# First values' projection: low parts of the weights on VectorE, one-column operations on ScalarE, the norm's factor in SBUF, other row products moved into the attention

## The chip, the cores and the metric

The kernel runs on one core of a Trainium2 chip. The metric is the device time of one execution in microseconds (us). A core has five queues that matter here: TensorE (PE: matrix products, and PEld, the loading of their stationary operand), VectorE (DVE), ScalarE (ACT), GpSimd (POOL) and SyncE (SP), which issues the transfers from the chip's memory (HBM). SBUF is the working memory; PSUM holds the results of TensorE, in eight banks of 512 float32 columns on 128 partitions each.

## The reference

A trunk of four layers over 512 positions and 1024 features, in float32. Every sub-layer normalizes its input, scales and shifts it by factors from a conditioning vector `c`, and adds a gated, normalized result. The first sub-layer, where this change lies, is attention with 16 heads of 64:

```python
mod_all = jnp.einsum('bd,lde->lbe', jax.nn.silu(c), w_mod) + b_mod[:, None, :]
...
sh_m, sc_m, g_m, sh_f, sc_f, g_f = jnp.split(mod_all[layer], 6, axis=-1)
u = modulate(rms_norm(h, norm_g[layer, 0]), sh_m, sc_m)
...
q, k, v = jnp.split(u @ w_qkv, 3, axis=-1)
```

with `modulate(h, shift, scale) = h * (1 + scale) + shift`. Behind it come the 16 heads (scores, a cumulative product along the keys, weighted values), the output projection, and a channel mixer.

## The kernel before

**Number format.** Each float32 operand of a large product is split in two parts, `hi` (rounded by ScalarE) and `lo` (the rest, a subtraction, `split`, L235 to L238). A product is then three matmuls: hi with hi, hi with lo, lo with hi (`mm3`, L219 to L222). Weights arrive in a tile `raw` (four buffers, one 512 KB transfer each, issued by SP) and are split into `whi` and `wlo`, or, in the spare form, into two chunks each of tag `x`. ScalarE makes the high part; the low part is made by GpSimd where `far` (L172 to L174) says so, otherwise by VectorE. While `starting` is set, `far` says GpSimd, and the split is made in two halves.

**Row products.** A block of 128 elements of `mod_all` is a product of the 128 rows of a transferred 128x1024 block with `c`, summed along the row, by one VectorE operation (`mod_block`, L371 to L376). It uses the same four `raw` buffers.

**The start.** The kernel forms the norm's factor R of the input (`pre_r`, `rstd`): squares, two float32 products with `ones_d` into an `aux` bank of PSUM, and four short operations, the last of which (L429) writes R over that same bank. Then, for each of 8 blocks k of 128 features (`prenorm`, L453 to L473): `first(k)` makes the two row products of the block (shift and scale) and `mod_pre` their four one-column operations on VectorE (L384 twice, L385, L387); the weights of block k are fetched and split; VectorE scales `t` = h times `apre` times R (L466); ScalarE makes the high part of u (L467) and VectorE the low part (L469).

**The values' projection** (`attention`, `mid`, L670 to L682) accumulates V = u @ w_v over the 8 blocks in eight accumulators at once, four of tag `mm` and four of tag `aux`, which are all eight banks of PSUM: 24 matmuls per block, 192 in all. After each of the first six blocks one task is taken from a list (`self.some(V_SOME[k])`): a row product that is needed only later. Then follow projections of queries and keys for head pairs (`q_block`, `k_block`), 24 matmuls each, and the loop over the heads (`sticks`, `flip`, `gather`), in which one further task is taken per round (L726) and the rest at its end.

**Order.** Each engine works through its queue in order. The queues are filled at build time by a scheduler that follows the code's order and dependencies; inside the head loop TensorE's order is written out (`ordered`).

Of the kernel before, what the change touches and what calls it, by code (L numbers as in the profile page):

```python
# [11 lines left out]
AF = mybir.ActivationFunctionType  # L12
ALU = mybir.AluOpType
# [4 lines left out]
KC = D // P  # L18
S = 512
# [3 lines left out]
HEADS = 16  # L23
# [4 lines left out]
QT = 4  # L28
N_WARM = 60
H_TB, H_H = 1, 0  # L30
V_SOME = (1, 1, 1, 1, 1, 1, 0, 0)
NB = S // QT
NPAIR = 32
FULL = slice(0, S)
# [44 lines left out]
class Trunk:  # L79
    def __init__(self, ctx, tc, ins, out):  # L80
        self.tc, self.nc, self.ins, self.out = tc, tc.nc, ins, out
        nc = self.nc
        pool = lambda **k: ctx.enter_context(tc.tile_pool(**k))
        self.const = pool(name="const", bufs=1)
        self.act = pool(name="act", bufs=1)
        self.wp = pool(name="wp", bufs=3)
        self.tmp = pool(name="tmp", bufs=2)
        self.mx = pool(name="mx", bufs=1)
        self.ps = pool(name="ps", bufs=4, space=bass.MemoryType.PSUM)
        self.dram = pool(name="dram", bufs=1, space=bass.MemoryType.DRAM)  # L90
        self.n = 0
        self.todo = []
        self.halves = {}
        self.crossing = False
        self.ordered, self.last, self.mark = False, None, None
        self.hold = None
        self.joint, self.clock, self.starting, self.near = False, 0.0, True, False

        self.cb = self.const.tile([P, D], F32, name="cb")
        nc.sync.dma_start(self.cb, ins["c"].to_broadcast([P, D]))  # L100
        self.h = self.const.tile([P, KC, S], F32, name="h")
        for k in range(KC):
            nc.sync.dma_start(self.h[:, k, :], ins["xT"][:, k, :])
        self.vec = self.const.tile([P, VCOLS], F32, name="vec")
        nc.sync.dma_start(self.vec, ins["vec"])
        nc.vector.tensor_scalar(self.v("ln_g"), self.v("ln_g"), -0.5, None, ALU.mult)

        self.ident = self.const.tile([P, P], F32, name="ident")
        make_identity(nc, self.ident)
        self.ident_b = self.const.tile([P, P], BF16, name="ident_b")  # L110
        nc.vector.tensor_copy(self.ident_b, self.ident)
        self.ones_d = self.const.tile([P, P], F32, name="ones_d")
        nc.vector.memset(self.ones_d, 1.0 / D)
        mask = self.const.tile([P, P], F32, name="mask")
        nc.vector.memset(mask, -1e30)
        nc.gpsimd.affine_select(out=mask, in_=mask, pattern=[[1, P]], compare_op=ALU.is_ge,
                                fill=0.0, base=0, channel_multiplier=-1)
        self.mask_b = self.const.tile([P, P], BF16, name="mask_b")
        nc.vector.tensor_copy(self.mask_b, mask)
        self.zero = self.const.tile([P, 1], F32, name="zero")  # L120
        nc.vector.memset(self.zero, 0.0)
        self.epsb = self.const.tile([P, 1], F32, name="epsb")
        nc.vector.memset(self.epsb, EPS)

        warm = self.psum("aux")
        for _ in range(N_WARM):
            nc.tensor.matmul(warm[:, :P], self.ident_b, self.mask_b, start=True, stop=True)
        sig = self.wp.tile([P, D], F32, tag="raw", bufs=4, name="sig")
        nc.scalar.activation(sig, self.cb, AF.Sigmoid)
        nc.vector.tensor_tensor(self.cb, self.cb, sig, ALU.mult)  # L130
        self.mod = [self.const.tile([P, 48], F32, name=f"mod{l}") for l in range(DEPTH)]
        self.apre = [self.const.tile([P, 2, KC], F32, name=f"apre{l}") for l in range(DEPTH)]
        self.gpost = [self.const.tile([P, 2, KC], F32, name=f"gpost{l}") for l in range(DEPTH)]
# [37 lines left out]

    def far(self, i):  # L172

        return self.starting or self.ordered and not self.near and (i or not self.crossing)  # L174

    def fetch(self, src):
        raw = self.wp.tile([P, D], F32, tag="raw", name=self.nm("raw"), bufs=4)
# [3 lines left out]
    def weights(self, src, spare=None, raw=None):  # L181

        n = src.shape[-1]
        if raw is None:
            raw = self.fetch(src)
        if spare:
            t = [[self.chunk(spare) for _ in range((n + S - 1) // S)] for _ in range(2)]
            for i, (hi, lo) in enumerate(zip(*t)):
                w = min(S, n - i * S)
                self.split(raw[:, i * S : i * S + w], hi[:, :w], lo[:, :w], self.far(i))  # L190
            cut = lambda t: [t[k // 4][:, (k % 4) * P : (k % 4 + 1) * P] for k in range(n // P)]
            return cut(t[0]), cut(t[1]), t
        hi = self.wp.tile([P, D], F32R, tag="whi", name=self.nm("whi"))
        lo = self.wp.tile([P, D], F32R, tag="wlo", name=self.nm("wlo"))
        if self.ordered or self.starting:
            for i, c in enumerate((slice(0, n // 2), slice(n // 2, n))):
                self.split(raw[:, c], hi[:, c], lo[:, c], self.far(i))
        else:
            self.split(raw[:, :n], hi[:, :n], lo[:, :n])
        cut = lambda t: [t[:, k * P : (k + 1) * P] for k in range(n // P)]  # L200
        wide = lambda t: [t[:, i * S : (i + 1) * S] for i in range(2)]
        return cut(hi), cut(lo), (wide(hi), wide(lo))
# [176 lines left out]
    def mod_pre(self, l, s, k=0, n=KC):  # L379
# [6 lines left out]
                                       self.v("norm_g", (l * 4 + 2 * s) * KC + k, n), ALU.add, ALU.mult)  # L386
        nc.vector.tensor_scalar(self.apre[l][:, s, k : k + n], self.apre[l][:, s, k : k + n], -0.5, None, ALU.mult)  # L387

    def mod_gate(self, l, s):
        nc = self.nc  # L390
        e = 24 * s + 16
        o = VOFF["b_mod"][0] + 48 * l + e
        g = self.gpost[l][:, s, :]
        nc.vector.tensor_tensor(g, self.mod[l][:, e : e + 8], self.vec[:, o : o + 8], ALU.add)
        nc.vector.scalar_tensor_tensor(g, g, -0.5, self.v("norm_g", (l * 4 + 2 * s + 1) * KC, KC),
                                       ALU.mult, ALU.mult)
# [55 lines left out]

    def prenorm(self, l, s, u, sl=FULL, before=None):  # L453
        nc = self.nc
        R, _ = yield from self.pre_r(sl)
        n = sl.stop - sl.start
        room = self.psum("aux") if n < S else None
        for k in range(KC):
            if before is not None:
                before(k)  # L460
            if sl.start == 0:
                u.append((self.chunk("u"), self.chunk("u")))
            hi, lo = u[k][0][:, sl], u[k][1][:, sl]
            a, b = self.apre[l][:, s, k : k + 1], self.mod[l][:, 24 * s + k : 24 * s + k + 1]
            t = self.scratch("t", sl) if room is None else room[:, k % 2 * n : (k % 2 + 1) * n]
            scale = nc.vector.scalar_tensor_tensor(t, self.h[:, k, sl], a, R, ALU.mult, ALU.mult)  # L466
            self.step = nc.scalar.activation(hi, t, AF.Identity, bias=b), scale  # L467
            if k % 2 == 0 or not self.crossing:
                nc.vector.scalar_tensor_tensor(lo, t, b, hi.bitcast(F32), ALU.add, ALU.subtract)  # L469
            else:  # L470
                x = self.scratch("t", sl)
                nc.scalar.activation(x, t, AF.Identity, bias=b)
                nc.gpsimd.tensor_tensor(lo, x, hi.bitcast(F32), ALU.subtract)  # L473
# [152 lines left out]
    def attention(self, l, j, first=None, spare=(), n_p=4):  # L626
        nc, ins = self.nc, self.ins
# [42 lines left out]
        def mid():  # L670
            v = [self.pairs("hid", 3) + [(self.chunk("hid", F32),)] for _ in range(2)]
            pss = [self.psum("aux" if i % 2 else "mm") for i in range(8)]
            for k in range(KC):
                if n_s:
                    wv.append(self.weights(ins["sb_w_v"][j, k]))
                hi, lo = wv[k][2]
                for tb in range(4):
                    ts = slice(tb * P, (tb + 1) * P)
                    for half in range(2):
                        self.mm3(pss[2 * tb + half], u[k][0][:, ts], u[k][1][:, ts], hi[half], lo[half],  # L680
                                 k == 0, k == KC - 1)
                self.some(V_SOME[k])  # L682
            self.starting = False
            todo = [proj(i) for i in range(n_s, HEADS)]
            self.load(todo[0])
# [14 lines left out]
            it, n = iter(()), 0  # L700
            for i in range(HEADS + 2):
# [7 lines left out]
                if todo:  # L709
                    b = todo.pop(0)  # L710
                    it, n = self.steps(b), b["srcs"][0].shape[-1] // P
# [10 lines left out]
                if i >= HEADS - 2:  # L722
                    while 2 * len(os) + 1 <= i - 2:
                        os.append((self.chunk("x"), self.chunk("x")))
                        self.split(o[len(os) - 1], *os[-1])
                self.some(1)  # L726
            self.several(it, 1)
            self.ordered = False
            self.rest()
# [553 lines left out]
    def run(self, subs=8):  # L1283
        nc = self.nc

        def first(k):
            if k == 1:
                self.mark, self.hold = self.step[1], self.step
            self.mod_block(0, k)
            self.mod_block(0, 8 + k)  # L1290
            self.mod_pre(0, 0, k, 1)

        ph = []
        for l in range(DEPTH):
# [113 lines left out]
```

## Time and profile before

| | us |
|---|---|
| three timed executions | 2680.76, 2685.21, 2686.60 |
| their median | 2685.21 |
| the profiled execution | 2679.98 |
| its span in the profile | 2678.3 |

The profiled execution is one more execution, not one of the three. Its span runs from the first to the last instruction in the trace. All times of the rows below count from the start of that span. In a row, "busy" is the time in which an engine worked; the clause in brackets is the idle time of the engine just before the instruction, and what ended it. `L216` is line 216 of the kernel; names such as `aux`, `u`, `raw` are those of the tiles.

### The profile page before, as it was taken

To read this page: it belongs to the slowest core of one execution; us is meant where nothing else is said; L and a number is where in the kernel's file an instruction comes from. 1 tells how busy PE (TensorE), PEld (TensorE's weight loads), DVE (VectorE), ACT (ScalarE), POOL (GpSimd) and SP (SyncE) were. 2 spreads that over 40 slices of the span, in tenths; PEclk is the share of its full clock that TensorE was granted. 3 is DMA by queue.
4 is the path that set the end of the run, shared out by engine and by line. 5 is a ranking of instruction groups with operands and counts; after the bars stand their busy time and mean duration, and the time that the engine had idled before them with its cause. 6 is when DMAs were issued, how large, how long until landed. Compare 5 with 4: busy or idle time off the path is not lost. (4 is left out here: it accounts for less than half of the span.)

```text
span 2678.3 us, 34946 instructions
## 1 busy us (share of the span) xinstructions
PE 2472.9 (92%) x12903; PEld 2062.1 (77%) x12903; DVE 1650.1 (62%) x2662; ACT 1197.1 (45%) x2323; POOL 694.7 (26%) x757
## 2 busy tenths in 40 slices
PE   6999899999858989999987879999999999999998
PEld 4776788777757888888876778888887777888887
DVE  8799667566669454555469965656354887522335
ACT  3577442434446553222365654222244776522222
POOL 3123312965335130000047751000031233200001
PEclk8999999999989999999998989999999999999999
DMA  7422216566735314754301121656221113022221
GB/s 262 145 91 98 98 65 211 165 208 231 283 106 178 108 42 149 244 188 171 120 32 48 63 71 57 231 192 220 98 92 63 48 44 114 33 95 93 94 99 53
DMA packets 115323, 335.06 MB, mean 125 GB/s; under 512 B 12112, under 2 KB 26960, under 8 KB 115152
## 3 DMA queue, kind: packets, MB, share of 16 engines
q1 hardware_dynamic: 115152, 332.84, 36.6%
q8 instruction: 101, 1.65, 0.2%
q14 instruction: 70, 0.57, 0.1%
HBM read 314.18 MB, written 18.61 MB: 124 GB/s over the span
## 5 line engine op out<-in xcount | busy, mean ns | idle before, releaser
L216 PE MATMUL mm<-u,whi 128*128 128x512 f32 (+1 forms) x3568 | 1071.4, 383 | 10.4 <-DVE cum L750 6.6
L216 PEld LDWEIGHTS mm<-u,whi 128*128 128x128 f32 x3568 | 655.1, 190 | 151.6 <-DVE cum L750 7.5
L237 ACT ACTIVATE whi<-raw 128x1024 fp32r<-128x1024 f32 (+3 forms) x392 | 344.3, 895 | 864.4 <-PE mm L216 528.5
L216 PE MATMUL mm<-u,wlo 128*128 128x512 f32 (+1 forms) x1784 | 683.9, 384 | 0.9 <-DVE wlo L238 0.8
L238 DVE TENSOR_TENSOR wlo<-raw,whi 128x1024 fp32r<-128x1024 f32 (+2 forms) x302 | 358.3, 1189 | 362.3 <-ACT whi L237 358.4
L216 PE MATMUL mm<-hid,whi 128*128 128x512 f32 (+1 forms) x1832 | 507.9, 365 | 12.9 <-ACT whi L237 10.4
L216 PEld LDWEIGHTS mm<-u,wlo 128*128 128x128 f32 x1784 | 337.6, 189 | 70.9 <-DVE wlo L238 2.2
L216 PEld LDWEIGHTS mm<-hid,whi 128*128 128x128 f32 x1832 | 330.0, 192 | 71.5 <-ACT whi L237 11.3
L216 PE MATMUL mm<-hid,wlo 128*128 128x512 f32 (+1 forms) x916 | 332.9, 364 | 2.1 <-DVE wlo L238 2.1
L443 POOL TENSOR_TENSOR acc<-acc,sq 128x256 f32<-128x256 f32 (+1 forms) x92 | 72.8, 791 | 805.1 <-ACT sq L442 803.7
L376 DVE SCALAR_TENSOR_TENSOR raw<-raw,cb 128x1024 f32<-128x1024 f32 x192 | 242.6, 1284 | 52.3 <-DMA raw<-in_w_modT_dram 51.3
L238 POOL TENSOR_TENSOR wlo<-raw,whi 128x512 fp32r<-128x512 f32 (+1 forms) x90 | 117.1, 1319 | 386.1 <-ACT whi L237 386.1
L500 DVE TENSOR_TENSOR g<-g,mm 128x512 f32<-128x512 f32 (+1 forms) x100 | 62.0, 623 | 233.5 <-PE mm L216 225.6
L216 PEld LDWEIGHTS mm<-hid,wlo 128*128 128x128 f32 x916 | 175.5, 192 | 31.3 <-DVE wlo L238 3.7
L216 PE MATMUL mm<-u,x 128*128 128x256 f32 (+1 forms) x832 | 131.6, 291 | 24.7 <-ACT u L467 6.6
L216 PE MATMUL mm<-hid,u 128*128 128x256 f32 x1104 | 144.9, 293 | 0.0
L216 PEld LDWEIGHTS mm<-hid,u 128*128 128x128 f32 x1104 | 142.0, 201 | 0.7
L216 PEld LDWEIGHTS mm<-u,x 128*128 128x128 f32 x832 | 113.2, 197 | 33.3 <-ACT u L467 8.0
L514 DVE TENSOR_TENSOR m<-mm,m 128x256 f32<-128x256 f32 (+1 forms) x92 | 48.1, 526 | 89.6 <-PE mm L216 89.4
L786 POOL TENSOR_TENSOR hid<-ident,hid 128x512 fp32r<-128x512 f32 (+1 forms) x17 | 19.2, 1145 | 309.4 <-ACT hid L237 307.9
L443 POOL TENSOR_TENSOR acch<-acch,sq 128x256 f32<-128x256 f32 x96 | 75.5, 787 | 58.1 <-ACT sq L442 56.5
L817 DVE SCALAR_TENSOR_TENSOR aux<-cum,vec,aux 128x512 f32<-128x512 f32 (+1 forms) x125 | 86.6, 709 | 2.6
(297 smaller groups left out, 3361.8 us busy)
## 6 DMA issues: line engine op xcount, KB each, us to landing
raw<-in_w_modT_dram SPq DMA_DIRECT2D x192, 512.0 KB, 4.3
raw<-in_ffn_w_gate_dram SPq DMA_DIRECT2D x88, 512.0 KB, 4.0
raw<-in_ffn_w_up_dram SPq DMA_DIRECT2D x88, 512.0 KB, 3.3
raw<-in_ffn_w_down_dram SPq DMA_DIRECT2D x64, 448.0 KB, 4.0
raw<-in_sb_w_qkv_dram SPq DMA_DIRECT2D x32, 512.0 KB, 3.3
raw<-in_ffn_w_down_dram SPq DMA_DIRECT2D x32, 512.0 KB, 4.5
raw<-in_cv_w_pw_dram SPq DMA_DIRECT2D x24, 512.0 KB, 3.2
s5tab<-x SPq DMA_DIRECT2D x40, 256.0 KB, 2.9
```

What stands on the lines that cost most here:

```text
L216: self.queue(self.nc.tensor.matmul(out, lhsT, rhs, **k))
L237: a = self.nc.scalar.activation(hi, src, AF.Copy)
L238: b = (self.nc.gpsimd if pool else self.nc.vector).tensor_tensor(lo, src, hi.bitcast(F32), ALU.subtract)
L376: self.after(nc.vector.scalar_tensor_tensor(raw, raw, 1.0, self.cb, ALU.mult, ALU.mult, accum_out=self.mod[l][:, e : e + 1]), self.mark)
L443: (nc.gpsimd if self.mark else nc.vector).tensor_tensor(acc, acc, sq, ALU.add)
L500: self.mark = nc.vector.tensor_tensor(g, g, pu, ALU.mult)
L514: nc.vector.tensor_tensor(m[ob][:, sl], ps, m[ob][:, sl], ALU.add)
L786: nc.gpsimd.tensor_tensor(d.rearrange("p (t c) -> p t c", t=n), self.ident.unsqueeze(1).to_broadcast([P, n, P]), w.bitcast(F32)[:, e - 2 * ...
L817: nc.vector.scalar_tensor_tensor(c, src(t), wd(k, t), c, ALU.mult, ALU.add)
```

## The change

Low parts of the weights in the first projection are made by VectorE, in one piece of 1024 columns (two of 512 in the spare form), as `starting` no longer counts in `far` and `weights`. The four one-column operations per block become two on ScalarE (`mod_first`), with the constants prepared for all blocks at once by two VectorE operations of 8 columns. For the whole-width norm R is written to a tile `g` in SBUF. The list `V_SOME` is gone: the values' projection takes no task, and the head loop takes two per round as long as more tasks are left than rounds.

```diff
+        g, b = self.v("norm_g", 0, KC), self.v("b_mod", 8, KC)
+        nc.vector.tensor_scalar(g, g, -0.5, None, ALU.mult)
+        nc.vector.scalar_tensor_tensor(b, b, 1.0, g, ALU.add, ALU.mult)
...
     def far(self, i):
-        return self.starting or self.ordered and not self.near and (i or not self.crossing)
+        return self.ordered and not self.near and (i or not self.crossing)
...
-        if self.ordered or self.starting:
+        if self.ordered:
             for i, c in enumerate((slice(0, n // 2), slice(n // 2, n))):
                 self.split(raw[:, c], hi[:, c], lo[:, c], self.far(i))
...
+    def mod_first(self, k):
+        nc = self.nc
+        a, b = (self.mod[0][:, e : e + 1] for e in (k, 8 + k))
+        nc.scalar.activation(a, a, AF.Identity, bias=self.v("b_mod", k))
+        nc.scalar.activation(self.apre[0][:, 0, k : k + 1], b, AF.Identity, scale=self.v("norm_g", k),
+                             bias=self.v("b_mod", 8 + k))
...
-        R, _ = yield from self.pre_r(sl)
         n = sl.stop - sl.start
+        R, _ = yield from self.pre_r(sl, self.t512("g") if n == S else None)
...
-                self.some(V_SOME[k])
...
-                self.some(1)
+                self.some(2 if len(self.todo) > HEADS + 1 - i else 1)
...
             self.mod_block(0, k)
             self.mod_block(0, 8 + k)
-            self.mod_pre(0, 0, k, 1)
+            self.mod_first(k)
```

What this does to the queues is shown at three places.

First place, the values' projection. TensorE's queue before, where the eighth accumulator (`aux_435`) gets its first matmul; `whi_226` and `u_232`, `u_233` are weights and u (high, low) of block 0, `whi_326` and `u_333` of the fifth block:

```order
L216 MATMUL mm_432<-whi_326,u_333 128x512
L216 MATMUL aux_433<-whi_326,u_333 128x512
L216 MATMUL mm_434<-whi_326,u_333 128x512
L216 MATMUL aux_435<-whi_226,u_232 128x512
L216 MATMUL aux_435<-wlo_227,u_232 128x512
L216 MATMUL aux_435<-whi_226,u_233 128x512
L216 MATMUL aux_435<-whi_250,u_256 128x512
```

and after, in block 0 (`whi_227`; `u_231` and `u_232` are now the high and low part of u in that block, `aux_414` is the eighth accumulator):

```order
L218 MATMUL aux_412<-wlo_228,u_231 128x512
L218 MATMUL mm_413<-whi_227,u_231 128x512
L218 MATMUL mm_413<-wlo_228,u_231 128x512
L218 MATMUL aux_414<-whi_227,u_231 128x512
L218 MATMUL aux_414<-wlo_228,u_231 128x512
L218 MATMUL mm_407<-whi_227,u_232 128x512
L218 MATMUL aux_408<-whi_227,u_232 128x512
L218 MATMUL mm_409<-whi_227,u_232 128x512
```

The eighth accumulator's matmuls have moved from behind the fifth block into each block. ScalarE's queue at the same place before, from the weights of block 0 to those of the third block (`raw_272`):

```order
L237 ACTIVATE whi_226<-raw_224 128x512 x2
L467 ACTIVATE u_232<-t_234,mod_171 128x512
L237 ACTIVATE whi_250<-raw_248 128x512 x2
L467 ACTIVATE u_256<-t_258,mod_171 128x512
L237 ACTIVATE x_274<-raw_272 128x512
L237 ACTIVATE x_275<-raw_272 128x512
L467 ACTIVATE u_282<-t_284,mod_171 128x512
```

and after:

```order
L239 ACTIVATE whi_227<-raw_225 128x1024
L477 ACTIVATE u_231<-t_233,mod_173 128x512
L395 ACTIVATE mod_173<-mod_173,vec 128x1
L239 ACTIVATE whi_247<-raw_245 128x1024
L396 ACTIVATE apre_177<-mod_173,vec 128x1
L395 ACTIVATE mod_173<-mod_173,vec 128x1
L239 ACTIVATE x_267<-raw_265 128x512
L477 ACTIVATE u_251<-t_253,mod_173 128x512
L239 ACTIVATE x_268<-raw_265 128x512
```

Two one-column rows per block (L395, L396) are new, and high parts of `whi` come in one row; the high part of u of block 1 (`u_256` before, `u_251` after) now has a one-column row of the third block and half of that block's weights ahead of it.

Second place, VectorE's queue in the second head of the attention, up to the low parts (`u`, `sq`, `wt`) that free the banks for the third head. Before:

```order
L586 SCALAR_TENSOR_TENSOR cum_881<-t_878,zero 128x255
L588 TENSOR_TENSOR w_863<-w_863,cum_881 128x255
L586 SCALAR_TENSOR_TENSOR cum_891<-g_888,zero 128x383
L588 TENSOR_TENSOR w_862<-w_862,cum_891 128x383
L560 TENSOR_TENSOR x_911<-mm_834,x_910 64x512
L586 SCALAR_TENSOR_TENSOR cum_901<-t_898,zero 128x511
L588 TENSOR_TENSOR w_862<-w_862,cum_901 128x511
L238 TENSOR_TENSOR u_943<-aux_937,u_942 128x512
L376 SCALAR_TENSOR_TENSOR raw_1358,mod_171<-raw_1358,cb 128x1024
L238 TENSOR_TENSOR sq_951<-aux_946,sq_950 128x384
L238 TENSOR_TENSOR wt_958<-aux_954,wt_957 128x256
L548 TENSOR_TENSOR x_1023<-mm_924,x_1023 64x512
```

After:

```order
L378 SCALAR_TENSOR_TENSOR raw_1206,mod_173<-raw_1206,cb 128x1024
L596 SCALAR_TENSOR_TENSOR cum_855<-g_852,zero 128x383
L404 TENSOR_TENSOR gpost_181<-mod_173,vec 128x8
L570 TENSOR_TENSOR x_875<-mm_795,x_874 64x512
L598 TENSOR_TENSOR w_826<-w_826,cum_855 128x383
L405 SCALAR_TENSOR_TENSOR gpost_181<-gpost_181,vec 128x8
L596 SCALAR_TENSOR_TENSOR cum_865<-t_862,zero 128x511
L240 TENSOR_TENSOR u_907<-aux_901,u_906 128x512
L598 TENSOR_TENSOR w_826<-w_826,cum_865 128x511
L240 TENSOR_TENSOR sq_915<-aux_910,sq_914 128x384
L240 TENSOR_TENSOR wt_922<-aux_918,wt_921 128x256
L378 SCALAR_TENSOR_TENSOR raw_1334,mod_173<-raw_1334,cb 128x1024
```

A row product (`raw_1206`) now stands inside the second head's scans, together with the gate's two operations (L404, L405), and the one that stood between `u` and `sq` (`raw_1358` before) has its like behind `wt`.

Third place, VectorE's queue in the last rounds of the head loop, from a head's longer scans to the low parts of its weights. Before:

```order
L586 SCALAR_TENSOR_TENSOR cum_2559<-g_2556,zero 128x383
L586 SCALAR_TENSOR_TENSOR cum_2569<-t_2566,zero 128x511
L588 TENSOR_TENSOR w_2530<-w_2530,cum_2559 128x383
L376 SCALAR_TENSOR_TENSOR raw_2864,mod_171<-raw_2864,cb 128x1024
L588 TENSOR_TENSOR w_2529<-w_2529,cum_2569 128x511
L376 SCALAR_TENSOR_TENSOR raw_2867,mod_171<-raw_2867,cb 128x1024
L238 TENSOR_TENSOR u_2618<-aux_2612,u_2617 128x512
L238 TENSOR_TENSOR sq_2626<-aux_2621,sq_2625 128x384
L238 TENSOR_TENSOR wt_2633<-aux_2629,wt_2632 128x256
```

After:

```order
L596 SCALAR_TENSOR_TENSOR cum_2547<-g_2544,zero 128x383
L596 SCALAR_TENSOR_TENSOR cum_2557<-t_2554,zero 128x511
L598 TENSOR_TENSOR w_2518<-w_2518,cum_2547 128x383
L598 TENSOR_TENSOR w_2517<-w_2517,cum_2557 128x511
L240 TENSOR_TENSOR u_2606<-aux_2600,u_2605 128x512
L240 TENSOR_TENSOR sq_2614<-aux_2609,sq_2613 128x384
L240 TENSOR_TENSOR wt_2621<-aux_2617,wt_2620 128x256
```

The two row products (`raw_2864`, `raw_2867`) are gone from here.

## Rows read from the trace of the kernel before

**Rows 1.** The page, part 1: busy time, share of the span, instructions.

```profile
PE 2472.9 (92%) x12903; PEld 2062.1 (77%) x12903; DVE 1650.1 (62%) x2662; ACT 1197.1 (45%) x2323; POOL 694.7 (26%) x757
```

**Rows 2.** Windows: stretch, length, busy per engine (instructions), granted clock, DMA share, GB/s.

```profile
21.60:52.40 30.80, 27.80 (x105) 20.82 (x105) 30.38 (x53) 7.90 (x13) 13.43 (x8) 0.93 0.74 256
52.40:60.40 8.00, 0.01 (x1) 0.00 (x0) 7.77 (x18) 3.02 (x5) 2.99 (x3) 0.78 0.76 249
60.40:82.00 21.60, 21.57 (x87) 17.56 (x88) 14.98 (x18) 6.69 (x10) 5.58 (x4) 0.92 0.67 248
...
19.00:60.00 41.00, 27.81 (x105) 20.82 (x105) 40.34 (x72) 11.26 (x19) 18.19 (x13) 0.88 0.70 239
```

**Rows 3.** Timeline of TensorE, first projection: start, length, instruction, out<-in, count.

```profile
21.65 0.80 PE L216 MATMUL mm<-whi,u 128*128 128x512 f32 x1 [5.40 <-ACT u L467]
...
26.09 0.44 PE L216 MATMUL aux<-whi,u 128*128 128x512 f32 x1
...
60.44 0.80 PE L216 MATMUL aux<-whi,u 128*128 128x512 f32 x1 [8.03 <-DVE t L466]
...
71.12 0.86 PE L216 MATMUL mm<-x,u 128*128 128x512 f32 x3
...
82.06 0.63 PE L216 MATMUL mm<-u,whi 128*128 128x512 f32 x2
```

**Rows 4.** Timeline of VectorE in the same stretch.

```profile
18.40 1.66 DVE L429 SCALAR_TENSOR_TENSOR aux<-u,u 128x512 f32<-128x512 f32 x1
...
42.24 1.77 DVE L469 SCALAR_TENSOR_TENSOR u<-t,mod,u 128x512 fp32r<-128x512 f32 x1
43.94 1.31 DVE L384 TENSOR_TENSOR mod<-mod,vec 128x1 f32<-128x1 f32 x2
...
47.47 1.22 DVE L376 SCALAR_TENSOR_TENSOR raw<-raw,cb 128x1024 f32<-128x1024 f32 x1
...
48.62 0.75 DVE L469 SCALAR_TENSOR_TENSOR u<-t,mod,u 128x512 fp32r<-128x512 f32 x1
49.28 0.22 DVE L384 TENSOR_TENSOR mod<-mod,vec 128x1 f32<-128x1 f32 x2
...
59.63 0.75 DVE L466 SCALAR_TENSOR_TENSOR t<-h,apre,aux 128x512 f32<-128x512 f32 x1
...
76.11 1.23 DVE L238 TENSOR_TENSOR wlo<-raw,whi 128x1024 fp32r<-128x1024 f32 x1 [2.50 <-ACT whi L237]
```

**Rows 5.** Timeline of GpSimd, 41 to 50 us.

```profile
41.56 3.60 POOL L238 TENSOR_TENSOR wlo<-raw,whi 128x512 fp32r<-128x512 f32 x2 [2.51 <-ACT whi L237]
```

**Rows 6.** Waits, 0 to 85 us: who for whom, us, times, longest.

```profile
ACT x L237 <- DMA raw<-in_sb_w_v_dram: 4.0, 2, 2.6
DVE raw L376 <- DMA raw<-in_w_modT_dram: 3.4, 4, 1.2
```

**Rows 7.** Groups of ScalarE, whole span: count, busy us, mean ns, idle before.

```profile
L918 ACT ACTIVATE x<-x 128x32 f32<-128x32 f32 x2 | 0.4, 214 | 0.0
```

**Rows 8.** Tile `raw`, 0 to 60 us: from issue to landing.

```profile
DMA to landing us min/median/max: 3.1/4.2/8.1
```

**Rows 9.** Timeline of TensorE in the attention.

```profile
119.08 1.01 PE L216 MATMUL aux<-x,x 128*128 128x384 f32 x2 [3.51 <-DVE sq L238]
...
273.44 0.80 PE L216 MATMUL aux<-x,x 128*128 128x256 f32 x2 [5.19 <-DVE u L238]
```

**Rows 10.** Timeline of VectorE at the attention's end.

```profile
261.60 1.67 DVE L376 SCALAR_TENSOR_TENSOR raw<-raw,cb 128x1024 f32<-128x1024 f32 x1 [1.23 <-DMA raw<-in_w_modT_dram]
...
268.76 1.22 DVE L376 SCALAR_TENSOR_TENSOR raw<-raw,cb 128x1024 f32<-128x1024 f32 x1
...
271.03 1.74 DVE L376 SCALAR_TENSOR_TENSOR raw<-raw,cb 128x1024 f32<-128x1024 f32 x1
```

**Rows 11.** Windows in the attention (columns as in rows 2).

```profile
119.10:121.00 1.90, 1.90 (x6) 1.07 (x7) 1.84 (x4) 0.75 (x2) 0.57 (x1) 0.50 0.74 248
...
165.00:187.00 22.00, 21.44 (x114) 16.41 (x114) 20.24 (x31) 16.38 (x39) 5.12 (x4) 1.00 0.28 96
```

More of the change, by code (lines that the diff above doesn't have):

```diff
@@ L30 @@
 H_TB, H_H = 1, 0
-V_SOME = (1, 1, 1, 1, 1, 1, 0, 0)
 NB = S // QT
```

## The prediction

> **What bounds the kernel now.** The page's busy table comes first: TensorE is busy for 92% of the span [rows 1]. A change elsewhere is worth what it takes from TensorE's other 8%, or from its time at low clock, so the question is where TensorE stands still around the first values' projection. The windows answer it: from 21.6 to 52.4 us TensorE is nearly always busy, from 52.4 to 60.4 not at all, while VectorE is full through all of it (40.34 of the 41 us from 19 to 60) [rows 2]. The timeline of TensorE says what ended the standstill: at 60.44 a product into an `aux` accumulator, released by VectorE's scaling `t` (L466), after 8.03 us [rows 3]. That scaling is the eighth and last, begun at 59.63 [rows 4]. A scaling does not make an accumulator, so why should a product wait for the last one? Because the norm's factor R lies in an `aux` bank. The projection wants all eight banks; seven are free early, the eighth holds R until the last block has been scaled. TensorE's queue shows the same: the eighth accumulator (aux_435) gets its first product only behind the seven others' fifth block. The reader is to see two things: a lack of room, not of work, made the 8 us; and all of the eighth accumulator's work was pushed behind it, so that the projection ran on until 82.06, where the first query product begins with no gap.
>
> The floor of the projection: it is 8 blocks of 24 products, 192. At full clock 48 of them take from 71.12 to 82.06, 0.228 us each. The first ten, at the start, take from 21.65 to 26.09, 0.444 each [rows 3]: the low level, after a time without work. So 60.4 us are spent on what needs 4.4 + 182 x 0.23 = 46.3.
>
> **The change, part by part.**
>
> (a) R in SBUF. The bank is free when the two short steps that make R have read it, before the first scaling. In the new queue the eighth accumulator's products stand in their place in each block. If nothing else is late, TensorE starts at 21.65 as before (R's chain is the same; the first weights' low part now stands ahead of the first scaling, 1.15, but the last step of R, held by GpSimd's first split to 1.66 for the 0.75 of its like, gives 0.9 of it back [rows 4]) and ends at 21.65 + 46.3 = 68.0, against 82.06: -14.
>
> (b) Can the others feed a block every 5.5 us (24 x 0.23)? VectorE per block now: two row products, 1.15 from start to start (47.47 to 48.62); scaling and low part of u, 0.66 each (48.62 to 49.28); the weights' low part, a row of 1.23 that by the same rule (its end overlaps the next start) is 1.15 [rows 4]. Together 2.3 + 1.3 + 1.15 = 4.8 a block, 38 us for eight, from about 19 us on: the last scaling falls near 57, and it may fall at 59.63 as before without harm: 0.75 for it, about as much for ScalarE's high part (an estimate from rows of that size), 5.5 of products gives 66.6, still under 68.0. What leaves VectorE: 32 one-column operations, two of which take 0.22 undisturbed and 1.31 when GpSimd works (43.94 against 49.28), and the conflicts: the low part of u takes 1.77 instead of 0.75 beside GpSimd's split of 41.56 [rows 4, 5]. GpSimd has nothing left to do here.
>
> ScalarE gets two one-column operations a block, 0.21 each by the nearest row (32 columns) [rows 7], and is busy for 11.26 of 41 us [rows 2]. But its order matters: u's high part stands behind a one-column operation that awaits a row product, and behind the next weights' high part, which awaits a transfer. Transfers had made ScalarE wait 4.0 us in two places and VectorE 3.4 in four [rows 6]. Three transfers a block pass through four buffers; each holds its buffer for the landing, 4.2 in the median [rows 8], and its use (1.15 for a row product, some 2.4 for weights): (3 x 4.2 + 2.3 + 2.4) / 4 = 4.3 us a block, under 5.5 with little more than a microsecond to spare. I take 1 us of waits in all: **-13**. Bounds: -14 as above; at 0.9 us short per block, -7.
>
> The Trainium skill (ScalarE: Activation LUTs, Rules for kernel authors) says that plain adds and multiplies belong on VectorE, and (What ACT_TABLE_LOAD costs) puts a one-column operation at 0.28 us with one operand per partition and 0.09 more with a second; both together would be 0.65 a block. No run here shows a one-column operation on ScalarE. Were all of it on u's way, the projection would end 5 us later, a gain of 8 in place of 13; I hold it for hidden, since TensorE's block is longer than VectorE's.
>
> (c) Six row products leave the projection. They ran after the last scaling, beside TensorE's late products, and cost TensorE nothing there; their six transfers make room for the query weights.
>
> (d) They return in the attention. It does 24 row products instead of 18, up to two per head for the first nine. By the queue's order the heads 1 to 6 hold eleven (five before): 6 x 1.15 = 6.9 us more of VectorE. Its cover: in a pair of heads (165 to 187 us) VectorE is busy 20.24 of 22.0 and TensorE 21.44 [rows 11], so VectorE has 1.76 us free per pair, some 5 us in three pairs, TensorE 0.56. Where VectorE is late, TensorE waits for it: 3.51 us at 119.08, before the third head, and then runs at low clock (0.50 granted, which is 1.2 GHz) [rows 9, 11]; in the new order three products fall just before that place. From below, all hidden: 0. From above, all exposed and a spell of low clock behind: 8. I take **+3**, nearer the covered end since most of the free time is usable.
>
> (e) At the attention's end before, four row products stood in heads 14 and 15, now one. The one at 261.60 waited 1.23 for its transfer and took 1.67, the one at 268.76 took 1.15, the one at 271.03 took 1.67 up to 272.70, where the split that TensorE awaits starts; TensorE stood for 5.19 and went on at 273.44 [rows 9, 10]. Some 5.7 us leave VectorE's way; TensorE can gain the 5.19 and the low clock behind (ten products at 0.444 for 0.23: 2.1). Bounds -1 and -7; I take **-5**, what TensorE waited.
>
> Sum: -13 + 3 - 5 = -15. The profiled execution took 2679.98: 2665. The three timed runs lie at 2680.8 to 2686.6 with a median 5.2 above it; against that median I expect **2670**.
>
> **Rivals.**
>
> *VectorE becomes the attention's bound, mildly.* GpSimd goes on splitting one weight block per head, and an added product that meets it takes longer: u's low part lost 1.02 to it (1.77 for 0.75) [rows 4]. Then the six cost 6 x (1.15 + 1.02) = 13, the projection's whole gain, and 2680 - 13 + 13 - 5 = 2675 (2680 against the median). The Trainium skill (SBUF — State Buffer, SBUF: two separate sides) states it as a rule: a VectorE operation with two SBUF inputs and a GpSimd operation that reads SBUF exclude each other for a whole instruction; the trace agrees (1.77 beside 0.75). Against it: not each product meets a split. Chance 13%.
>
> *The same, in full: slower.* If each of the six also brings TensorE a spell of low clock (2.1), they cost 6 x 4.3 = 26: -13 + 26 - 5 = +8, 2688 (2693). It decides from 3.9 us a product on. For it: 119.08, where a wait brought the clock down. Against: the free time above, and waits of about half a microsecond per pair at 165 to 187 left the clock at 1.00 [rows 11]. Chance 4%.
>
> *Transfers become the pace.* If the landing rises to the 8.1 of the worst transfer [rows 8], a block needs (24.3 + 4.7) / 4 = 7.25 us; TensorE waits in every block and starts each at low clock (4.4 + 14 x 0.23 = 7.7), the projection ends near 83, and (d) and (e) leave 2679 (2684): no change. For it: the shape of ScalarE's queue. Against: the median, and six transfers fewer. Chance 7%.
>
> *The projection gains only 8* (ScalarE's small operations exposed): 2670 (2675). Chance 6%.
>
> **How the numbers follow.** The forecast, -10 to -20, has 70%. A measurement of this kernel can tell about 0.2%, 5.4 us, from no change. Faster: the forecast, the small gain (6%), and half of the mild rival and of the transfers' (10): 86%. Within 0.2%: the other half of these two: 10%. Slower: 4%. The forecast alone spans 2660 to 2675; with 1 to 7 us between profile and runs, and the mild rival, 2659 to 2680.
>
> **What would show it.** Right: no wait of TensorE above 2 us between its first projection product and the first query product, the latter near 69 us; GpSimd idle until the projections that follow; the 5.19 us wait of the attention's end gone. Wrong: TensorE waiting for u in each block (ScalarE behind a transfer or a row product); waits for VectorE's splits in heads 1 to 6 above 10 us in sum; low granted clock there; the query product at 75 us or later.

## The result, and the profile after

The kernel after takes 2671.11 us (median of six executions, 2665.30 to 2675.40); six executions of the kernel before have a median of 2685.90 (2680.76 to 2689.32). The ratio after to before is 0.9944, with a 95% interval of 0.9928 to 0.9960: faster, by 15 us. The profiled execution has a span of 2663.6 us, 14.7 less than before.

The page's busy table and then the windows of the kernel after, at the stretches of [rows 2]:

```profile
PE 2472.4 (93%) x12903; PEld 2061.3 (77%) x12903; DVE 1641.7 (62%) x2644; ACT 1199.8 (45%) x2335; POOL 673.2 (25%) x741
```

```profile
21.60:52.40 30.80, 30.80 (x126) 24.92 (x127) 29.00 (x47) 13.34 (x27) 0.00 (x0) 0.93 0.90 306
52.40:60.40 8.00, 8.00 (x36) 6.49 (x35) 5.99 (x9) 3.83 (x6) 0.00 (x0) 1.00 0.93 299
60.40:82.00 21.60, 21.60 (x95) 17.52 (x94) 15.51 (x20) 9.55 (x15) 2.37 (x2) 1.00 0.44 143
19.00:60.00 41.00, 38.65 (x159) 31.31 (x160) 37.60 (x57) 17.89 (x34) 0.00 (x0) 0.92 0.87 290
```

TensorE's total is as before [rows 1]; what went is standing time. From 52.4 to 60.4 it is now busy all through, GpSimd does nothing, and VectorE still has 37.60 us of work in 41. TensorE's timeline (the rows that answer to [rows 3] and [rows 9]):

```profile
21.35 0.79 PE L218 MATMUL mm<-whi,u 128*128 128x512 f32 x1 [5.44 <-ACT u L477]
...
67.70 0.63 PE L218 MATMUL mm<-u,whi 128*128 128x512 f32 x2
...
107.25 0.79 PE L218 MATMUL aux<-x,x 128*128 128x256 f32 x2 [5.06 <-DVE u L240]
...
133.75 0.50 PE L218 MATMUL aux<-x,x 128*128 128x256 f32 x2 [1.85 <-DVE u L240]
...
251.34 0.80 PE L218 MATMUL aux<-x,x 128*128 128x256 f32 x2 [4.04 <-DVE u L240]
```

The first query product begins at 67.70 instead of 82.06, with no wait in the projection. The wait before the third head's scores, 3.51 at 119.08 in before [rows 9], is now 5.06; the 5.19 of 273.44 has no successor (the 4.04 at 251.34 answers a 3.39 at 258.43 in before).

Four landmarks locate the gain in every kernel: the first query product (Q), and the starts of VectorE's low parts `wt` (the last split that a head's weights need) of the first, twelfth and last of the 16 heads, in us; the two differences are the early attention and its end. "Before 2" and "after 2" are second profiles of the same kernels; the other names are explained below.

| kernel | Q | first | twelfth | last | Q to twelfth | twelfth to last | span |
|---|---|---|---|---|---|---|---|
| before | 82.06 | 118.95 | 246.72 | 289.16 | 164.7 | 42.4 | 2678.3 |
| before 2 | 83.72 | 120.61 | 245.69 | 288.40 | 162.0 | 42.7 | 2687.6 |
| after | 67.70 | 108.47 | 238.99 | 275.81 | 171.3 | 36.8 | 2663.6 |
| after 2 | 67.59 | 108.08 | 238.56 | 275.33 | 171.0 | 36.8 | 2666.0 |
| R alone | 78.18 | 117.83 | 242.90 | 282.46 | 164.7 | 39.6 | 2673.6 |
| R back | 77.04 | 115.90 | 245.11 | 281.77 | 168.1 | 36.7 | 2672.9 |
| low parts back | 70.75 | 111.53 | 238.99 | 275.45 | 168.2 | 36.5 | 2665.9 |
| one-column back | 75.39 | 115.57 | 246.05 | 283.18 | 170.7 | 37.1 | 2670.5 |
| rows back | 68.23 | 105.23 | 233.09 | 272.43 | 164.9 | 39.3 | 2660.6 |
| six, 3 double | 69.05 | 110.11 | 233.69 | 270.49 | 164.6 | 36.8 | 2662.5 |
| eight | 71.83 | 113.44 | 239.13 | 276.12 | 167.3 | 37.0 | 2667.6 |
| eight, 1 double | 72.59 | 110.89 | 234.27 | 270.95 | 161.7 | 36.7 | 2666.4 |
| seven, 2 double | 69.52 | 107.66 | 231.24 | 268.03 | 161.7 | 36.8 | 2659.2 |
| six, 0/4/6 double | 68.53 | 105.94 | 230.76 | 267.50 | 162.2 | 36.7 | 2662.6 |

From before to after: -14.4 at Q, +6.6 up to the twelfth head, -5.6 at the end, -1.3 in all that follows.

### The profile page after: what moved, and what is told of

Read it like the earlier page. It is cut to its first block, busy times and chain, and to the rows that moved or that the text cites. A ratio compares the mean times of both kernels' runs of the same rounds, so it can differ in the third digit from the quotient of the medians.

```text
span 2663.6 us, 34918 instructions
## 1 busy us (share of the span) xinstructions
PE 2472.4 (93%) x12903; PEld 2061.3 (77%) x12903; DVE 1641.7 (62%) x2644; ACT 1199.8 (45%) x2335; POOL 673.2 (25%) x741
## 5 line engine op out<-in xcount | busy, mean ns | idle before, releaser
L240 POOL TENSOR_TENSOR wlo<-raw,whi 128x512 fp32r<-128x512 f32 (+1 forms) x82 | 104.3, 1288 | 419.0 <-ACT whi L239 419.0
```

The costliest lines, as they stand in the source:

```text
L240: b = (self.nc.gpsimd if pool else self.nc.vector).tensor_tensor(lo, src, hi.bitcast(F32), ALU.subtract)
```

## The experiments

**R alone.** The kernel before, and of the change only:

```diff
-        R, _ = yield from self.pre_r(sl)
+        R, _ = yield from self.pre_r(sl, self.t512("g") if sl.stop - sl.start == S else None)
```

> The kernel before with one edit: the norm's factor R goes to a tile in SBUF. Theory (the missing bank is what made TensorE stand): VectorE's scalings come 5.1 us apart as before, the last at about 59.6, so TensorE can work through the eight blocks nearly without a gap; the first query product begins at 67 to 70 instead of 82.06, and the span is 10 to 14 us shorter than 2678.3 (2664 to 2668), ratio about 0.995. Rival (VectorE's load and its conflicts with GpSimd are as much the cause): u comes late in each block, TensorE waits for it several times over 1 us and falls to the low clock; the query product begins at 74 or later and the span is at most 7 us shorter.

Median 2677.82, ratio 0.9973 (0.9962 to 0.9984). Q fell by 3.9 only: the rival's picture. TensorE's timeline, then VectorE's over one block:

```profile
45.06 0.50 PE L216 MATMUL mm<-x,u 128*128 128x512 f32 x1 [1.17 <-DVE u L469]
51.43 0.51 PE L216 MATMUL mm<-whi,u 128*128 128x512 f32 x1 [1.29 <-DVE u L469]
57.80 0.50 PE L216 MATMUL mm<-whi,u 128*128 128x512 f32 x1 [0.96 <-DVE u L469]
...
78.18 1.22 PE L216 MATMUL mm<-u,whi 128*128 128x512 f32 x2 [3.27 <-DVE hid L238]
```

```profile
49.62 1.76 DVE L469 SCALAR_TENSOR_TENSOR u<-t,mod,u 128x512 fp32r<-128x512 f32 x1
51.30 1.31 DVE L384 TENSOR_TENSOR mod<-mod,vec 128x1 f32<-128x1 f32 x2
52.64 0.16 DVE L385 SCALAR_TENSOR_TENSOR apre<-mod,vec 128x1 f32<-128x1 f32 x1
...
53.03 0.75 DVE L466 SCALAR_TENSOR_TENSOR t<-h,apre,g 128x512 f32<-128x512 f32 x1
...
55.98 1.76 DVE L469 SCALAR_TENSOR_TENSOR u<-t,mod,u 128x512 fp32r<-128x512 f32 x1
```

VectorE is the pace: 55.98 - 49.62 = 6.36 us a block, above the 5.5 of 24 products. Of these some 2.1 are time lost beside GpSimd's splits (1.76 for 0.75, 1.31 for 0.22, [rows 4]). The bank's wait was gone and another took its place; 3.27 of Q are V's splits, late behind the six row products.

**R back.** The kernel after with R in PSUM:

```diff
-        R, _ = yield from self.pre_r(sl, self.t512("g") if n == S else None)
+        R, _ = yield from self.pre_r(sl)
```

> The kernel after with R back in the PSUM bank. Theory (the bank): TensorE again stands until the last scaling, now at about 57.6 instead of 59.6, and the eighth accumulator's products run behind it; the first query product begins near 80, 12 us later than in the kernel after, span 2674 to 2677, hardly better than before. Rival (the relief of VectorE counts by itself): the query product begins at 74 or earlier and at least half of the 14.7 us stays.

Median 2677.77, ratio 0.9967 (0.9954 to 0.9979). The last scaling and the end of TensorE's wait, then the last scaling in after:

```profile
54.58 0.74 DVE L476 SCALAR_TENSOR_TENSOR t<-h,apre,aux 128x512 f32<-128x512 f32 x1
```

```profile
55.38 0.80 PE L218 MATMUL aux<-whi,u 128*128 128x512 f32 x1 [6.14 <-DVE t L476]
```

```profile
57.58 0.74 DVE L476 SCALAR_TENSOR_TENSOR t<-h,apre,g 128x512 f32<-128x512 f32 x1
```

The standstill returns, ended by the last scaling, as the bank theory says. But Q is 77.04, not 80: the last scaling begins at 54.58, earlier than the 57.58 that was expected from after, as fewer of the weights' low parts stand ahead of it. From the last scaling to Q it is 22.46 us here and 22.43 in before (59.63 to 82.06; 23.45 in the second profile of before): with R in the bank the projection ends a nearly fixed time behind VectorE's last scaling, so what the relief gives (5.0) shows in full. Neither theory had the size right.

**Low parts back** and **one-column operations back**, each undone alone in the kernel after:

```diff
-        return self.ordered and not self.near and (i or not self.crossing)
+        return self.starting or self.ordered and not self.near and (i or not self.crossing)
...
-        if self.ordered:
+        if self.ordered or self.starting:
```

> The kernel after with the low parts of the first projection's weights back on GpSimd, in two halves; R in SBUF and the one-column operations on ScalarE stay. Theory (by the kernel that had R alone, VectorE beside GpSimd's splits is what keeps u late): u's low part takes 1.76 instead of 0.75 in most blocks, but VectorE has 1.15 per block less to do, so it stays below TensorE's 5.5 us; the first query product begins 1 to 3 us later than 67.7, and the span is 1 to 3 us longer than after. Rival (moving the low parts carries most of the relief): VectorE's scalings come 6 us or more apart, the query product begins at 72 or later.

```diff
-            self.mod_first(k)
+            self.mod_pre(0, 0, k, 1)
```

(and without the two operations of 8 columns).

> The kernel after with the four one-column operations per block back on VectorE. Theory: without GpSimd beside them they take about 0.22 each, 0.9 a block, so VectorE needs 4.8 + 0.9 = 5.7 us a block against TensorE's 5.5; TensorE waits a little in late blocks, the query product begins 1 to 3 us later than 67.7, span 1 to 3 us longer than after. Rival (VectorE's chain from row product to scaling is what paces each block, and small operations cost more than their own time there): scalings 6.3 us apart as in the kernel with R alone, query product at 73 or later, span 5 us or more longer.

Low parts back: median 2667.62, ratio 0.9950 (0.9935 to 0.9964); Q 3.05 later, at the edge of what was expected. One-column operations back: median 2672.17, ratio 0.9960 (0.9947 to 0.9974); Q 7.7 later, the rival's size but not by its cause. Neither interval can be told from after's: what each of these two parts gives is seen at Q and not in the time. The operations are short (0.15 each without GpSimd); what changes is the order in two queues. VectorE's timeline, ScalarE's, and what TensorE then waits for:

```profile
20.24 0.75 DVE L473 SCALAR_TENSOR_TENSOR t<-h,apre,g 128x512 f32<-128x512 f32 x1
...
26.46 1.23 DVE L375 SCALAR_TENSOR_TENSOR raw<-raw,cb 128x1024 f32<-128x1024 f32 x1
...
29.82 1.22 DVE L375 SCALAR_TENSOR_TENSOR raw<-raw,cb 128x1024 f32<-128x1024 f32 x1
...
31.05 0.74 DVE L473 SCALAR_TENSOR_TENSOR t<-h,apre,g 128x512 f32<-128x512 f32 x1
```

```profile
32.82 0.63 ACT L236 ACTIVATE x<-raw 128x512 fp32r<-128x512 f32 x1 [3.88 <-DMA raw<-in_sb_w_v_dram]
33.36 0.71 ACT L474 ACTIVATE u<-t,mod 128x512 fp32r<-128x512 f32 x1
```

```profile
34.12 0.80 PE L215 MATMUL mm<-whi,u 128*128 128x512 f32 x1 [4.56 <-ACT u L474]
```

The second scaling begins at 31.05; in after it begins at 25.69. Two more row products, of later blocks, stand ahead of it in VectorE's queue. That scaling ends at 31.79, but the high part of u, which TensorE awaits, begins only at 33.36: in ScalarE's queue it stands behind a high part of the fourth block's weights, whose transfer ends a wait of 3.88 at 32.82 (in after the third block's stands there, at 27.50). So the last thing that held TensorE is a transfer, by ScalarE's order; an earlier scaling alone would not have freed it. Once past it, TensorE waits no more up to Q: of the 7.7, a later start has 0.45, this wait 4.56, and the rest goes with the low clock that follows it (0.53 granted from 34.12 to 40; the product at 34.12 lasts 0.80, like the first one at 21.35). The rows show the order of the queues as what costs here, not the load; that the small operations brought this order wasn't tried apart.

**Rows back** (list as before) and **six, 3 double** (list as before in the projection, the new rule in the head loop; it then doubles the first three rounds):

```diff
+V_SOME = (1, 1, 1, 1, 1, 1, 0, 0)
...
+                self.some(V_SOME[k])
...
-                self.some(2 if len(self.todo) > HEADS + 1 - i else 1)
+                self.some(1)
```

(the last pair of lines only in rows back).

> The kernel after with the list of row products as before: six in the first projection, one per round in the heads. Theory (the prediction's: the six cost nothing behind the last scaling): the first query product stays at 67.7; by the two traces the early heads then win back about 6.6 us and the attention's end loses 5.6, so 2662.5, the same as after within 2 us; the wait for VectorE near the attention's end is again about 5 us. Rival (their cover is gone): TensorE's late products of the eighth accumulator no longer lie there, so that six products, some 7 to 12 us of VectorE and its transfers behind 60 us, hold up the splits of V; TensorE waits 3 us or more for a bank before or in the first query products, and the span is 3 to 8 us longer than after.

> The kernel after with six row products in the first projection, and the new rule of the head loop (two per round as long as more tasks are left than rounds), which then doubles only the first three rounds. Theory (places count, each product in the second to fifth head costs about what it lasts): the early heads lose some 2 to 3 us instead of 6.6 and the end's gain of 5.6 stays, so 3 to 5 us shorter than after, 2659 to 2661. Rival (cover gone in the projection, as above): first query product 3 us or more late and no gain.

Rows back: median 2664.19, ratio 0.9927 (0.9914 to 0.9941). Six, 3 double: 2663.68, ratio 0.9916 (0.9902 to 0.9929). Rows back in VectorE's timeline, then TensorE's:

```profile
64.04 1.22 DVE L379 SCALAR_TENSOR_TENSOR raw<-raw,cb 128x1024 f32<-128x1024 f32 x1
...
67.49 1.28 DVE L241 TENSOR_TENSOR hid<-mm,hid 128x512 fp32r<-128x512 f32 x2
```

```profile
68.23 0.73 PE L219 MATMUL mm<-u,whi 128*128 128x512 f32 x2
...
103.38 0.50 PE L219 MATMUL aux<-x,x 128*128 128x256 f32 x2 [1.90 <-DVE u L241]
```

The six products end at 65.2 and V's first split starts at 67.49, just in time: TensorE goes on at 68.23 with no wait (its first product is 0.4 later, too). So the cover in the projection holds for six, and the heads are back to 164.9: moving the row products cost 6.4 us there. The rival of lost cover falls. At the end rows back still gains 3.1 on before, although its list is before's; the wait of about 5 us that was expected there is 2.23. Its last `wt` comes at 272.43, 3.4 ahead of after's: by the landmarks, moving the row products as this change does was a loss. Six, 3 double fell short of its 2659 to 2661 (span 2662.5): its early heads lose nothing against before (164.6) instead of 2 to 3, but Q is 1.4 later than in after.

**Eight**, **eight, 1 double**, **seven, 2 double** and **six, 0/4/6 double** move the tasks (the row products) further; the edits are given against rows back:

```diff
-V_SOME = (1, 1, 1, 1, 1, 1, 0, 0)
+V_SOME = (1, 1, 1, 1, 1, 1, 1, 1)
...
-                self.some(1)
+                self.some(2 if i == 0 else 1)
```

(the first pair alone is eight; seven has `(1, 1, 1, 1, 1, 1, 1, 0)` and `i < 2`, the last one the list of six and `i in (0, 4, 6)`).

> After, with eight row products in the first projection and one task per round in the heads. Theory (row products behind the last scaling are free as long as V's splits are not late, and each in the heads costs about what it lasts): two more than in the kernel with six end some 2.3 us later on VectorE (about 67.5 instead of 65.2), the first query products wait up to 1 us for their weights' low part, and the end of the attention has two fewer: 1 to 3 us shorter than the kernel with six (2660.6), 2658 to 2660. Rival (the cover ends at six): TensorE waits 2 us or more at the first query products and the span is the same as with six, or longer.

> After, with eight row products in the first projection and two tasks in the first round only, one in each other. Theory: the second task of the first round falls before the first head's scans, where VectorE still waits for others, and costs nothing; the last row product leaves the attention's end: 0 to 1.5 us shorter than the kernel with eight. Rival (it delays the queries' and keys' evictions): 1 us or more longer than the kernel with eight, with waits of TensorE between 85 and 110 us.

> After, with seven row products in the first projection and two tasks in each of the first two rounds. From the third round on the tasks stand as in the kernel with eight and a double first round, whose heads were the quickest (198.4 us from the first query product to the last head's `wt`, against 208.1 in after), but whose first query product waited 3.4 us. Theory: one product fewer behind the last scaling, 1.15 us, takes the wait down to 2 us or less, and the heads take 199 to 202: 2659 to 2663. Rival (the early product just moves into the first head and costs there): no better than the kernel with six, 204 us in the heads and 2661 or more.

> After, with six row products in the first projection and two tasks in the rounds 0, 4 and 6 only. Theory (crowding, not the number, is what costs in the early heads): no wait at the first query products, the early heads as in the kernel with six in the projection and one per round, about 1.15 us more for each doubled round that is not hidden, and the end as in after: 201 to 204 us from the query product to the last `wt`, 2658 to 2662. Rival (each product in rounds 4 and 6 costs 2 us and more, low clock included): 205 us or more, 2663 or more.

Medians 2667.41, 2666.13, 2662.10 and 2662.81; ratios 0.9941 (0.9928 to 0.9955), 0.9935 (0.9922 to 0.9948), 0.9924 (0.9912 to 0.9936) and 0.9924 (0.9912 to 0.9935). TensorE at Q, with eight and with seven:

```profile
71.83 1.22 PE L219 MATMUL mm<-u,whi 128*128 128x512 f32 x2 [3.45 <-DVE hid L241]
```

```profile
69.52 0.73 PE L219 MATMUL mm<-u,whi 128*128 128x512 f32 x2 [1.77 <-DVE hid L241]
```

Six products wait 0, seven 1.77, eight 3.45: behind the sixth, each costs 1.7. So eight missed its theory (a wait of up to 1) and bore out its rival, that the cover ends at six; seven, and eight with one double round, came out near their theories; 0/4/6 beat its 201 to 204 us from Q to the last `wt` (199.0), but not the time that went with it (2658 to 2662). The number in the heads, on the other hand, isn't what counts there: three more than in rows back, put into rounds 0, 4 and 6, make the early heads not slower (162.2 against 164.9) and the end as quick as after (36.7). Last `wt` at 267.50: 8.3 earlier than in after. Six with three doubles, seven with two and six with 0/4/6 can't be told apart by their intervals; each lies below that of after taken once more (0.9939 to 0.9963, next), and seven and six with 0/4/6 hold the earliest last `wt`.

**Before and after once more.**

> The kernel before once more, for a second profile. Theory (part of the gain at the attention's end was an accident of the first profile, since the kernels with the row products as before, R alone or with all else changed, needed 39.3 to 39.6 us from `wt` of the twelfth head to `wt` of the last, against its 42.4): 39 to 40 us. Rival (the long wait there belongs to the kernel before): 42 us or more.

> The kernel after once more, timed beside the others of this group, for a second profile. If what the two profiles showed is the kernel's and not one execution's: first query product at 67 to 68.5, from there to the low part `wt` of the last head 206 to 209 us (208.1 in the first profile), median about 2669 to 2672. If the rest of the span is what wanders: the time differs by up to 5 us with these two stretches unchanged.

After again: median 2669.48, ratio 0.9951 (0.9939 to 0.9963), and its landmarks repeat within 0.5 us. Before again: one time of 2689.31; the stretch at the end takes 42.7 again, so the theory of an accident falls and the long wait belongs to the kernel before. What differs is VectorE's queue. R alone at the end, VectorE's timeline and then TensorE's:

```profile
267.23 0.68 DVE L238 TENSOR_TENSOR u<-aux,u 128x512 fp32r<-128x512 f32 x1
...
268.29 1.21 DVE L376 SCALAR_TENSOR_TENSOR raw<-raw,cb 128x1024 f32<-128x1024 f32 x1
```

```profile
267.96 0.67 PE L216 MATMUL aux<-x,x 128*128 128x384 f32 x2 [2.30 <-DVE u L238]
```

In before the like row product stands at 271.03 [rows 10], ahead of the split `u` at 272.70. In R alone, with the same list, the build has put it behind `u`, TensorE waits 2.30 instead of 5.19, and the stretch takes 39.6.

## Why the prediction was right, and where its terms were not

*The place and the mechanism* held. TensorE stood for want of a bank: with R put back, it stands again, and the last scaling ends it.

*(a) and (b), -13:* measured -14.4. From TensorE's first product to Q it is 46.35 us; the working had 46.3 as the floor, and the 1 us of waits I added didn't come. VectorE's work was sized well: last scaling "near 57", at 57.58; "38 us for eight blocks", 37.60 busy in 41. The division between (a) and (b) was softer than the working reads: -14 stood for the bank "if nothing else is late", and without the relief something is, in block after block. R alone gives 3.9 at Q, all but R gives 5.0, both together 14.4.

*ScalarE's one-column operations* were under-priced, 0.21 by a row of 32 columns. The groups of after:

```profile
L396 ACT ACTIVATE apre<-mod,vec 128x1 f32<-128x1 f32 x8 | 3.0, 374 | 0.0
L395 ACT ACTIVATE mod<-mod,vec 128x1 f32<-128x1 f32 x8 | 2.4, 295 | 12.5 <-DVE raw L378 12.5
```

0.295 with one operand per partition and 0.374 with two, 0.67 a block: the trace agrees with the Trainium skill (ScalarE: Activation LUTs, What ACT_TABLE_LOAD costs), which gives 0.28 and 0.09 more. That they are hidden held: ScalarE waits 12.5 us for row products ahead of them, and no product of the projection waits.

*Transfers* did not become the pace: landing 3.2/4.6/8.2 (min, median, max) for [rows 8]'s 3.1/4.2/8.1. ScalarE waited 7.6 us for V's weights in six places, off TensorE's path.

*(c), 0:* right, and in rows back the cover is used to its last microsecond, which the text had not seen: a seventh product there costs 1.77.

*(d), +3: this is the term that was mis-sized.* It cost 6.6 up to the twelfth head (6.4 by rows back, 9.0 between the second profiles; 3.4 to 6.0 by R back, low parts back and one-column operations back, which have after's list, against before's first profile). In the stretch that was priced it cost more. The gathering of the sixth head's result on TensorE, in before and in after:

```profile
180.34 0.86 PE L216 MATMUL mm<-u,hid 128*64 128x512 f32 x3
```

```profile
175.34 0.86 PE L218 MATMUL mm<-u,hid 128*64 128x512 f32 x3
```

From Q that is 98.3 and 107.6: 9.3 lost, above the bound of 8, of which the seventh head gives 2.7 back (why was not tried). Two steps failed. The count: six more products in the attention and, by (e), three fewer at its end are nine more ahead of it, not six; between Q and the `wt` of the sixth head VectorE has 18 in after, 9 in before and in rows back. And the cover, "nearer the covered end since most of the free time is usable". VectorE before the first head's `u`, which frees a bank for the third head's scores, in after:

```profile
85.52 1.23 DVE L378 SCALAR_TENSOR_TENSOR raw<-raw,cb 128x1024 f32<-128x1024 f32 x1 [0.65 <-DMA raw<-in_w_modT_dram]
...
88.95 1.22 DVE L378 SCALAR_TENSOR_TENSOR raw<-raw,cb 128x1024 f32<-128x1024 f32 x1 [0.76 <-DMA raw<-in_w_modT_dram]
...
97.25 1.21 DVE L378 SCALAR_TENSOR_TENSOR raw<-raw,cb 128x1024 f32<-128x1024 f32 x1
...
101.79 1.23 DVE L378 SCALAR_TENSOR_TENSOR raw<-raw,cb 128x1024 f32<-128x1024 f32 x1 [0.74 <-DMA raw<-in_w_modT_dram]
...
106.50 0.69 DVE L240 TENSOR_TENSOR u<-aux,u 128x512 fp32r<-128x512 f32 x1
...
122.70 1.23 DVE L378 SCALAR_TENSOR_TENSOR raw<-raw,cb 128x1024 f32<-128x1024 f32 x1 [2.66 <-DMA raw<-in_w_modT_dram]
```

Four products ahead of `u`, and 2.15 us in which VectorE stands for their transfers: its free time is spent on their late data. (In rows back one product stands there, `u` comes 4.4 us sooner behind Q, and TensorE waits 1.90 and 1.41 for `u` and `sq` instead of 5.06 and 0.43.) Up to the sixth head these waits of VectorE, the one at 122.70 among them, sum to 9.45 in after and 2.16 in before. TensorE waits 5.06 for that `u`, and the stretch from 100 to 120 us has a granted clock of 0.74. TensorE's waits for VectorE's splits in heads 1 to 6 sum to 9.6: the prediction's own sign of being wrong, above 10, was nearly reached. The free time that [rows 11] show lies in a later pair of heads, and was carried to a place with less. The mild rival (13) saw that the added products would cost more than their own time, but by GpSimd's splits: these lengthen four of the 18 products (1.49 to 2.19 for 1.22), 3.0 us in sum, less than the transfers take.

*(e), -5:* measured -5.6, but on two legs. Some 3 hung on the place of one row product, ahead of `u` or behind it, and R alone and rows back, both with before's list, were built with it behind; 2.5 to 2.8 came from the products that left.

*The sum* of -15 met -14.7 because the errors, -1.4, +3.6, -0.6 and -1.3 in the rest of the span, nearly cancel: that the time came out so close is luck, not the working. The rest wanders by more than that, as the two profiles of before show.

## What to carry to other kernels

When a resource holds an engine back, ask whether its feeder could keep up if the resource were there: here bank and feeder each gave 4 to 5 us alone and 14 together. Price a moved operation at its new place in the queue, transfers included, not by the free time of the engine on average. And when most of a wait is one instruction standing ahead of the one that is awaited, expect any rebuild to move it.

## What the runs showed of the hardware

Two profiles of the same kernel before agree within 2 us at each landmark up to the last head, 289.16 and 288.40, and end 9.3 apart (2678.3 and 2687.6). By the starts of VectorE's like instructions the second is 0.3 ahead at 430 to 490 us and 8.8 behind at 910 to 970. The two of after part by 2.9 behind the last `wt`. Which transfers or clock steps do it was not tried; it sets how finely kernels of this length compare by one profile, and it is why the landmarks rather than the spans carry the argument above.
